# Two more places for expert weights and a 128-row product of the keys' low part, in a two-block transformer kernel

## The chip, the cores and the metric

One Trainium2 chip, one of its cores. The metric is the device time of one execution of the whole program, in microseconds (us); the median of three runs is given for the kernel before. TensorE is called PE below, its weight load PEld, VectorE DVE, ScalarE ACT, GpSimd POOL, and the queue of SyncE, which issues nearly all transfers, SP.

## The reference

256 tokens of width 1024 go through two different transformer blocks, all in float32. What matters here, cut to its core:

```python
# first block: mixer (8 heads + convolution), memory attention, then 32 experts
x = x + parallel_mixer(...); x = x + memory_cross_attention(...)
x = x + hierarchical_moe(h, ...)      # group by softmax, top 2 of its 8 experts
#   every expert: (silu(t @ wg) * (t @ wu)) @ wd, wg and wu 1024x512, wd 512x1024
x = rmsnorm(x, final_g)
# second block: HGRN2 mixer and sparse attention (16 heads of 64, 4 of keys), then
merged = sigmoid(ga) * (y_a @ w_branch_a) + sigmoid(gb) * (y_b @ w_branch_b)
h = h + rms_norm(merged @ w_out, ...)          # then a feed-forward layer and a gated input
# its selected and its window branch, at this length:
s = einsum('bgrqd,bgkd->bgrqk', q_rot, k)      # causal, softmax, times v
```

## The kernel before

The order of the work on each engine is set when the program is built, by a scheduler that gives each tile its place in SBUF and adds the waits; every engine, SP among them, then runs its own list in order. Each part of the first block and of the second is a product of 256 tokens with a weight matrix that arrives in pieces of 1 MB.

**Dense products** (`dense_nat`, `dense_T`). A piece of weights goes to a place of the pool `ring` (4 places), and `wsplit` (L184, L185) turns it into a high part `wh` (ACT, a cast to fp32r) and a low part `wl` (DVE, the rest) in the pool `hl` (3 places of each). The tokens are split the same way (`xTh`, `xTl`). A product is then three fp32r products, high by high, high by low and low by high, all through the helper at L195.

**The experts** (`moe_plan`, `mload`, `moe`). The experts' weights (192 pieces of 1 MB, in groups of four experts: 8 gate, 8 up and 8 down pieces) are used as they come, with no split. `moe_plan` lists the pieces in the order of use, and one row of `final_g` stands in the last group. `mload` puts piece number i into slot i modulo the number of slots. The slots are opened one after another as the first block ends and its tiles go: `NRB` places when the mixer's early tiles are gone, the 4 of `ring`, then `NR2`, `NRC`, `NRE` places, the 3 of `hl` (each holds a piece as two halves, named `wh` and `wl` here too, 512 KB each), and last `NRD`. With 8, 4, 2, 2, 2, 3 and 1 there are 22. The first 22 pieces are therefore loaded while the first block still computes, and each later one when the piece that holds its slot has been used. A product of four experts runs as four column strips (`bg`), and `gather` (`sp`) collects the tokens of the next four. Once, before the second group's loads go on, all engines pass a branch on the number of overflowing tokens (`nov`, L1059 to L1077); the branch holds the only transfers that GpSimd issues at addresses known at run time, and it isn't entered here.

**The second attention** (`att`, within `nsa`). For each of the 16 heads and each half of the queries (`hf`), one PSUM tile `tr` takes the scores of both branches, with 128 keys per branch for the first half and 256 for the second (so 256 and 512 columns). A key tile holds the head's 64 dimensions twice, on partitions 0 to 63 and 64 to 127; `kh` is the high part and `kl` the low part, each copied to the other half by L1503 and L1504. A query tile `qr` holds the high part of the query on one half of the partitions and its low part on the other. Three products go to `tr`:

```python
rr = slice(64 * j, 64 * j + 64)
self.mm(sc, q, kh[g // 2][:, g % 2, :, :kb], True, False)            # 128 rows: (qh + ql) . kh
self.mm(sc, q[rr], kl[g // 2][rr, g % 2, :, :kb], False, False)      # 64 rows: qh . kl
self.mm(sc[:, :, kb - 128:], self.idr, self.cnr[...], False, True)   # causal mask
```

`exps` then takes the maximum (DVE, `anm`) and the exponential (ACT, `P`), `turn` transposes `P` on PE (`hp`, L1547), and `values` multiplies by the values (`po`). The scores of head h, the transposes of head h-1 and the values of head h-2 are written together, and the scheduler sets dense products of the gates and branches between them.

Of the kernel before, what the change touches and what calls it, by code (L numbers as in the profile page):

```python
# [26 lines left out]
WARM = (5, 6, 0, 4, 8, (0, 2, 2, 2), 2, 4)  # L27
PIECES = ((0, 512), (512, 512)), ((0, 512), (512, 256), (768, 256))
ENG = ("VA", "PP", "VA", "VA")
NRB, NR2, NRC, NRE, NRD = 8, 2, 2, 2, 1  # L30
NS4, NPM, NPT, NPA, NHP = 16, 3, 2, 1, 2
ATT = 1300
NHV = 2
# [104 lines left out]
class B:  # L138
# [1212 lines left out]
    def nsa(self, uT, W, s4, b2):  # L1351
        tc, nc, A = self.tc, self.nc, self.A
# [95 lines left out]
        for hf in range(2):  # L1448
            sc = self.pat.tile([128, 16, 15], F32, name="po")
# [32 lines left out]
        kh, kl = ([s4(n, [128, 2, 2, S], F32R) for _ in range(2)] for n in ("kh", "kl"))  # L1482
        vv = []
        for br in range(2):
# [9 lines left out]
            for g2 in range(2):  # L1494
# [3 lines left out]
                for j in range(2):  # L1498
                    r, q = slice(64 * j, 64 * j + 64), slice(64 - 64 * j, 128 - 64 * j)
# [10 lines left out]
        for c, ps in turned(qn):  # L1510
            for j in range(2):
                r, q = slice(64 * j, 64 * j + 64), slice(64 - 64 * j, 128 - 64 * j)
# [4 lines left out]
        def att(ap, pax):  # L1517

            acc, Ps, PTs = {}, {}, {}

            def scores(h):
                g, j = h // 4, h % 2
                if not j:
                    acc[h // 2] = (self.pat.tile([128, 2, 2, 2, 64], F32, name="po"),
                                   self.sm.tile([128, 2, 2, 2], F32, name="asm", bufs=3))
                sm = acc[h // 2][1]
                nm = self.sm.tile([128, 2, 2], F32, name="anm", bufs=2)
                P = Ps[h] = ap.tile([128, 2, 384], F32, name="P", bufs=2)  # L1530
                rr = slice(64 * j, 64 * j + 64)
                for hf, kb, c0 in ((0, 128, 0), (1, 256, 128)):
                    sc = self.ptr.tile([128, 2, kb], F32, name="tr")
                    q = qr[g][:, h % 4, hf * 128:(hf + 1) * 128]
                    self.mm(sc, q, kh[g // 2][:, g % 2, :, :kb], True, False)
                    self.mm(sc, q[rr], kl[g // 2][rr, g % 2, :, :kb], False, False)
                    self.mm(sc[:, :, kb - 128:], self.idr,
                            self.cnr[:, None, :].to_broadcast([128, 2, 128]), False, True)
                    self.exps(sc, P[:, :, c0:c0 + kb], kb, nm[:, hf, :], sm[:, hf, :, j])

            def turn(h):
                P = Ps.pop(h)
                PT = PTs[h] = ap.tile([128, 2, 384], F32, name="PT", bufs=2)
                for br in range(2):
                    pt = pax.tile([128, 384], F32, name="hp")
                    for b in range(3):
                        nc.tensor.transpose(pt[:, b * 128:(b + 1) * 128], P[:, br, b * 128:(b + 1) * 128], idn)  # L1547
                    (V.tensor_copy if br else nc.scalar.copy)(PT[:, br, :], pt)

            def values(h):  # L1550
                g, j = h // 4, h % 2
                po, sm = acc[h // 2]
                PT = PTs.pop(h)
                for br in range(2):
                    v = lambda m: vv[br][:, m, g * 64:(g + 1) * 64]
                    self.mm(po[:, 0, br, j, :], PT[:, br, 0:128], v(0), True, True)
                    self.mm(po[:, 1, br, j, :], PT[:, br, 128:256], v(0), True, False)
                    self.mm(po[:, 1, br, j, :], PT[:, br, 256:384], v(1), False, True)
                if not j:
                    return  # L1560
                rc = self.sm.tile([128, 2, 2, 2], F32, name="arc", bufs=2)
                V.reciprocal(rc, sm)
                V.tensor_tensor(rc, rc, gn[:, :, 1:3, h - 1:h + 1], op=OP.mult)
                tt = self.sm.tile([128, 2, 2, 128], F32, name="att", bufs=2)
                V.tensor_tensor(tt.rearrange("p a b (j d) -> p (a b j) d", j=2), po.rearrange("p a b j d -> p (a b j) d"),
                                rc.rearrange("p a b j -> p (a b j)")[:, :, None].to_broadcast([128, 8, 64]), op=OP.mult)
                for hf in range(2):
                    y = yb[hf][:, (h - 1) * 64:(h + 1) * 64]
                    for br in range(2):
                        V.tensor_tensor(y, y, tt[:, hf, br], op=OP.add)  # L1570

            for h in range(18):
                if h < 16:
                    scores(h)
                if 0 < h <= 16:
                    turn(h - 1)
                if h > 1:
                    values(h - 2)
# [131 lines left out]
```

## Time and profile before

| what | value |
|---|---|
| time, median of 3 runs | 1335.99 us (1333.78 to 1336.66) |
| the profiled execution's own time | 1335.2 us |
| its span | 1333.4 us |
| PE busy | 1222.0 us (92%) |
| DVE, ACT busy | 609.2 us (46%), 482.4 us (36%) |
| data moved | 332.38 MB, 249 GB/s over the span |
| experts' stage | about 280 to 714 us |
| second attention | about 953 to 1058 us |

The span is that of the profiled execution, from its first to its last instruction; its own time lies 1.8 us above it. PE's busy time is partly modelled, so it is read together with the chain of waits, which says what each stretch of the end time hung on.

### The profile page before, as it was taken

The page shows a single profiled execution, that of the slowest core. Times are in us where ns is not written, and L with a number is a line of the kernel's source. Part 1 is how long each engine was busy: PE and PEld are TensorE (multiplying, and loading weights), DVE is VectorE, ACT ScalarE, POOL GpSimd, SP SyncE. Part 2 cuts the span into 40 slices and gives each one's busy share as a digit, 9 for nine tenths or more (in the row PEclk, how much of TensorE's full clock was granted, in tenths as well). Part 3 has the DMA queues.
Part 4 walks back from the last instruction along what each step waited for, and adds up shares of the span by engine and source line. Part 5 has one row for each costly group of instructions (what it writes and reads, how often), then busy time and mean ns, then how long its engine had stood idle before and what let it go on. Part 6 is the DMA issues. An engine that isn't in the chain of part 4 may idle for free.

```text
span 1333.4 us, 17835 instructions
## 1 busy us (share of the span) xinstructions
PE 1222.0 (92%) x7122; PEld 882.0 (66%) x7122; DVE 609.2 (46%) x1031; ACT 482.4 (36%) x916; POOL 130.0 (10%) x171
## 2 busy tenths in 40 slices
PE   8889999989978788796968999999999999999997
PEld 7779888844432323141414998888777878989886
DVE  5897655510100000010004677767656667564665
ACT  5676644300000000000004542345655446454553
POOL 3877000000000000000000000015000000000000
PEclk8999999989999898998989999999999999999999
DMA  8333595769999999999998444633521336555551
GB/s 282 127 127 127 199 379 196 299 249 417 421 417 420 419 417 420 417 420 418 417 407 309 159 158 127 204 129 105 179 95 64 105 132 213 184 196 178 202 190 48
DMA packets 106744, 332.38 MB, mean 249 GB/s; under 512 B 6368, under 2 KB 20512, under 8 KB 86176
## 3 DMA queue, kind: packets, MB, share of 16 engines
q1 hardware_dynamic: 106096, 329.87, 65.7%
q10 hardware_dynamic: 560, 1.31, 0.4%
q8 instruction: 58, 0.95, 0.3%
q14 instruction: 30, 0.25, 0.1%
HBM read 330.11 MB, written 1.05 MB: 248 GB/s over the span
## 4 chain that ended last, share of the span: by engine, by line
PE 48%; DMA 28%; ACT 1%; DVE 1%; issue 0%; DVEq 0%; POOLq 0%; SPq 0%; ACTq 0%
PE mm L195 29%; DMA w<-w_up_in 8%; DMA w<-w_down_in 8%; DMA w<-w_gate_in 7%; PE z L195 7%; PE bg L195 3%; DMA wh<-w_up_in 3%; PE po L195 2%; PE hp L195 2%; PE tr L195 2%; DMA wh<-w_gate_in 1%; PE sp L195 1%; PE hp L1547 1%; DMA w<-w_in_in 0%; ACT wh L184 0%
## 5 line engine op out<-in xcount | busy, mean ns | idle before, releaser
L185 DVE TENSOR_TENSOR wl<-w,wh 128x1024 fp32r<-128x1024 f32 (+2 forms) x228 | 278.9, 1238 | 158.6 <-ACT wh L184 157.4
L184 ACT CAST wh<-w 128x1024 fp32r<-128x1024 f32 (+2 forms) x228 | 235.6, 1044 | 201.7 <-PE mm L195 154.0
L195 PE MATMUL bg<-w,xs 128*32 128x512 f32 x888 | 172.9, 668 | 60.7 <-DMA w<-w_up_in 36.4
L195 PE MATMUL mm<-xTh,wl 128*128 128x256 f32 x688 | 195.6, 289 | 11.1 <-DVE wl L185 11.1
L195 PE MATMUL mm<-xTh,wh 128*128 128x256 f32 x688 | 190.2, 289 | 5.3 <-ACT wh L184 2.8
L195 PE MATMUL mm<-xTl,wh 128*128 128x256 f32 x688 | 193.3, 287 | 0.2 <-DVE xTl L253 0.2
L195 PE MATMUL mm<-wl,xTh 128*128 128x512 f32 (+1 forms) x440 | 173.1, 396 | 0.3 <-DVE wl L185 0.3
L195 PE MATMUL mm<-wh,xTh 128*128 128x512 f32 (+1 forms) x440 | 168.4, 401 | 4.3 <-ACT wh L184 1.3
L195 PE MATMUL mm<-wh,xTl 128*128 128x512 f32 (+1 forms) x440 | 170.3, 394 | 0.0
L195 PEld LDWEIGHTS bg<-w,xs 128*32 128x32 f32 x888 | 38.2, 119 | 179.5 <-issue 77.9
L195 PEld LDWEIGHTS mm<-xTh,wl 128*128 128x128 f32 x688 | 132.5, 193 | 14.1 <-DVE wl L185 13.5
L195 PEld LDWEIGHTS mm<-xTh,wh 128*128 128x128 f32 x688 | 129.6, 193 | 7.9 <-ACT wh L184 3.3
L195 PEld LDWEIGHTS mm<-xTl,wh 128*128 128x128 f32 x688 | 131.8, 193 | 0.8 <-DVE xTl L253 0.4
L988 DVE SCALAR_TENSOR_TENSOR sg<-bg,rsl,sg 128x512 f32<-128x512 f32 x8 | 6.0, 751 | 254.9 <-PE bg L195 254.9
L195 PEld LDWEIGHTS mm<-wh,xTh 128*128 128x128 f32 x440 | 82.4, 189 | 21.9 <-ACT wh L184 1.8
L195 PEld LDWEIGHTS mm<-wl,xTh 128*128 128x128 f32 x440 | 83.1, 189 | 18.0 <-DVE wl L185 1.9
L195 PEld LDWEIGHTS mm<-wh,xTl 128*128 128x128 f32 x440 | 83.0, 189 | 17.8 <-issue 0.7
L195 PE MATMUL bg<-w,ht 128*32 128x512 f32 x456 | 80.0, 598 | 3.5 <-DMA w<-w_down_in 2.8
L195 PEld LDWEIGHTS sp<-oh,X 128*128 128x128 f32 x256 | 61.5, 328 | 12.7 <-issue 10.9
L195 PE MATMUL sp<-oh,X 128*128 128x128 f32 x256 | 65.0, 403 | 0.0
L463 POOL TENSOR_TENSOR zc<-zc,zt 128x256 f32<-128x256 f32 x60 | 63.1, 1052 | 17.3 <-ACT zt L460 12.6
L996 ACT COPY ht<-sp 128x512 f32<-128x512 f32 x8 | 4.7, 586 | 139.8 <-PE sp L994 139.8
(414 smaller groups left out, 1538.2 us busy)
## 6 DMA issues: line engine op xcount, KB each, us to landing
w<-w_down_in SPq DMA_DIRECT2D x73, 1024.0 KB, 16.2
w<-w_up_in SPq DMA_DIRECT2D x68, 1024.0 KB, 15.0
w<-w_gate_in SPq DMA_DIRECT2D x59, 1024.0 KB, 19.9
w<-w_in_in SPq DMA_DIRECT2D x41, 1024.0 KB, 5.3
w<-w_mkv_in SPq DMA_DIRECT2D x8, 1024.0 KB, 5.0
w<-w_out_in SPq DMA_DIRECT2D x8, 1024.0 KB, 5.1
wh<-w_up_in SPq DMA_DIRECT2D x12, 512.0 KB, 17.5
wl<-w_up_in SPq DMA_DIRECT2D x12, 512.0 KB, 13.9
```

The lines of the kernel that those rows point to most:

```text
L184: self.nc.scalar.copy(hv, raw[:, j:j + g, :])
L185: self.nc.vector.tensor_tensor(lv, raw[:, j:j + g, :], hv.bitcast(F32), op=OP.subtract)
L195: return self.nc.tensor.matmul(out, lhsT, rhs, start=start, stop=stop, skip_group_check=True)
L463: nc.gpsimd.tensor_tensor(zi, zi, t, op=OP.add)
L988: V.scalar_tensor_tensor(sg, ps, rsl[q], sg, op0=OP.mult, op1=OP.mult)
L996: nc.scalar.copy(ht, tp)
L1547: nc.tensor.transpose(pt[:, b * 128:(b + 1) * 128], P[:, br, b * 128:(b + 1) * 128], idn)
```

## The change

Two edits. `NRB` goes from 8 to 9 and `NRD` from 1 to 2, so there are 24 slots in place of 22, which is just the number of pieces of four experts; the room comes from a smaller scratch for dynamic transfers. And the score product with the keys' low part takes all 128 rows, which adds the product of the query's low part with the key's low part to the scores.

```diff
-NRB, NR2, NRC, NRE, NRD = 8, 2, 2, 2, 1
+NRB, NR2, NRC, NRE, NRD = 9, 2, 2, 2, 2
...
-                rr = slice(64 * j, 64 * j + 64)
...
-                    self.mm(sc, q[rr], kl[g // 2][rr, g % 2, :, :kb], False, False)
+                    self.mm(sc, q, kl[g // 2][:, g % 2, :, :kb], False, False)
...
-    nc = bacc.Bacc("TRN2", target_bir_lowering=False, num_devices=1)
+    nc = bacc.Bacc("TRN2", target_bir_lowering=False, num_devices=1, dynamic_dma_scratch_size=1024)
```

Lists of DVE and ACT are the same in both kernels; PE's list differs only within the experts' stage, where the down products meet other tiles first. In the second attention no instruction moves on any engine. SP's list of transfers is shown at three places. The first is where the last pieces of the first group are loaded and the first slots are used again, just ahead of the branch (L1059). Before, with two down pieces that wait for PE to give slots back:

```order
L868 DMA wl<-w_down_in 128x1024 [waits DMAHW0_49,PE_49]
L868 DMA w<-w_down_in 128x2048 [waits DMAHW1_49,PE_49]
L868 DMA wh<-w_down_in 128x1024 [waits DMAHW2_49]
L868 DMA w<-w_down_in 128x2048 [waits DMAHW3_49,PE_49]
L868 DMA w<-w_down_in 128x2048 [waits DMAHW4_49,PE_49]
L868 DMA w<-w_gate_in 128x2048 [waits DMAHW5_49,PE_49]
L868 DMA w<-w_gate_in 128x2048 [waits DMAHW6_49,PE_49]
L1059 TENSOR_LOAD nov [waits DVE_49]
```

Now the same place reads:

```order
L868 DMA wl<-w_down_in 128x1024 [waits DMAHW1_49,PE_49]
L868 DMA w<-w_down_in 128x2048 [waits DMAHW2_49,PE_49]
L868 DMA w<-w_down_in 128x2048 [waits DMAHW3_49]
L868 DMA wh<-w_down_in 128x1024 [waits DMAHW4_49]
L868 DMA w<-w_gate_in 128x2048 [waits DMAHW5_49,PE_49]
L868 DMA w<-w_gate_in 128x2048 [waits DMAHW6_49,PE_49]
L868 DMA w<-w_gate_in 128x2048 [waits DMAHW7_49,PE_49]
L868 DMA w<-w_gate_in 128x2048 [waits DMAHW0_49,PE_49]
L1059 TENSOR_LOAD nov [waits DVE_49]
```

All down pieces of the first group now stand ahead of the first reused slot, and the four loads ahead of the branch are the next group's gate pieces. The second place is SP's list where the memory attention's output weights (`w_mo`) are loaded, in the first block. Before:

```order
L868 DMA w<-w_gate_in 128x2048 [waits DMAHW3_49]
L868 DMA w<-w_gate_in 128x2048
L868 DMA w<-w_gate_in 128x2048 [waits DMAHW5_49,PE_49]
L167 DMA w<-w_mo_in 128x4x512 [waits DMAHW6_49,PE_49]
L167 DMA w<-w_mo_in 128x4x512 [waits DMAHW7_49,PE_49]
```

And now, with the ninth early place filled first:

```order
L868 DMA w<-w_gate_in 128x2048 [waits DMAHW3_49]
L868 DMA w<-w_gate_in 128x2048 [waits Pool_49]
L868 DMA w<-w_gate_in 128x2048 [waits DMAHW5_49,PE_49]
L868 DMA w<-w_up_in 128x2048 [waits DMAHW6_49]
L167 DMA w<-w_mo_in 128x4x512 [waits DMAHW7_49,PE_49]
L167 DMA w<-w_mo_in 128x4x512 [waits DMAHW0_49]
```

One more piece of the experts stands ahead of `w_mo`. The third place is SP's list at the end of the experts' stage, with the last down pieces and the first weights of the second block (`w_in`). Before:

```order
L868 DMA w<-w_down_in 128x4x512 [waits DMAHW2_49,PE_49]
L167 DMA w<-w_in_in 128x4x512 [waits DMAHW3_49,PE_49]
L167 DMA w<-w_in_in 128x4x512 [waits DMAHW4_49,PE_49]
L167 DMA w<-w_in_in 128x4x512 [waits DMAHW5_49,PE_49]
L1374 DMA w_5335<-cmp_wk_2_in 128x2x64 [waits DMAHW2_49,DMAHW1_49,DMAHW6_49,DMAHW0_49,PE_49]
L1374 DMA w_5335<-cmp_wv_2_in 128x2x64 [waits DMAHW7_49]
L167 DMA w<-w_in_in 128x4x512 [waits DVE_49]
```

And now:

```order
L868 DMA w<-w_down_in 128x4x512 [waits DMAHW2_49,PE_49]
L167 DMA w<-w_in_in 128x4x512 [waits DMAHW3_49,PE_49]
L167 DMA w<-w_in_in 128x4x512 [waits DMAHW4_49,PE_49]
L167 DMA w<-w_in_in 128x4x512 [waits DMAHW5_49,PE_49]
L167 DMA w<-w_in_in 128x4x512 [waits DMAHW6_49,PE_49]
L1374 DMA w_5335<-cmp_wk_2_in 128x2x64 [waits DMAHW1_49,DMAHW7_49,DMAHW0_49,PE_49]
L1374 DMA w_5335<-cmp_wv_2_in 128x2x64
```

The fourth `w_in` piece no longer waits for DVE, since with 24 slots the row of `final_g` and the last down pieces no longer end up in `ring`; the last pieces that `ring` holds are up pieces.

## Rows read from the trace of the kernel before

**Rows 1.** Busy time by stretch: engines' us (instructions), granted PE clock, DMA share, GB/s.

```profile
203.00:230.00 27.00, 26.95 (x168) 24.51 (x167) 15.42 (x25) 10.99 (x23) 0.00 (x0) 1.00 0.41 144
262.00:278.00 16.00, 16.00 (x96) 11.77 (x98) 5.59 (x30) 1.80 (x4) 0.00 (x0) 1.00 0.13 52
...
300.00:690.00 390.00, 324.03 (x1665) 122.56 (x1669) 23.93 (x46) 15.03 (x27) 0.00 (x0) 0.95 1.01 418
```

**Rows 2.** SP's transfers in order of time: start, us, engine, line, tile.

```profile
188.04 1.27 SPq L167 DMA_DIRECT2D w<-w_mo_in  x2
...
255.94 0.44 SPq L868 DMA_DIRECT2D wh<-w_down_in  x1
278.45 0.80 SPq L868 DMA_DIRECT2D w<-w_down_in  x2
...
700.14 9.48 SPq L167 DMA_DIRECT2D w<-w_in_in  x3
```

**Rows 3.** SP's own waits, 250 to 280 us, then 300 to 730 us: total, times, longest.

```profile
SPq L868 <- PE bg L195: 22.1, 1, 22.1
...
SPq L868 <- PE bg L195: 9.5, 19, 2.2
```

**Rows 4.** Transfers by tile: count, KB each, median us to landing.

```profile
w<-w_down_in SPq DMA_DIRECT2D x73, 1024.0 KB, 16.2
```

**Rows 5.** The chain that ended last, at the end of the experts' stage: start, us.

```profile
697.66 15.42 DMA w<-w_down_in
```

**Rows 6.** ACT in order of time: the first casts of `w_mo` and of `w_in`.

```profile
220.94 2.00 ACT L184 CAST wh<-w 128x1024 fp32r<-128x1024 f32 x2
...
716.02 1.99 ACT L184 CAST wh<-w 128x1024 fp32r<-128x1024 f32 x2 [1.18 <-DMA w<-w_in_in]
```

**Rows 7.** Busy time in the second attention, columns as in Rows 1.

```profile
953.50:1058.50 105.00, 105.00 (x576) 82.79 (x575) 59.48 (x121) 57.64 (x170) 0.00 (x0) 1.00 0.27 91
```

**Rows 8.** The chain that ended last, 950 to 1070 us: shares by line, and one piece.

```profile
by line: PE mm L195 48.6%; PE tr L195 23.3%; PE po L195 16.7%; PE hp L1547 8.8%; PE mm L298 1.5%; PE tr L298 1.3%
...
955.30 4.64 PE mm L195 x20
```

**Rows 9.** PE in order of time, one head's scores: start, us, out<-moving,stationary.

```profile
953.42 0.28 PE L195 MATMUL tr<-kh,qr 128*128 128x256 f32 x1
953.63 0.38 PE L195 MATMUL tr<-kl,qr 64*128 64x256 f32 x1
953.94 0.38 PE L195 MATMUL tr<-cnr,idr 128*128 128x256 f32 x1
954.16 0.40 PE L195 MATMUL tr<-kh,qr 128*128 128x512 f32 x1
954.49 0.49 PE L195 MATMUL tr<-kl,qr 64*128 64x512 f32 x1
954.91 0.39 PE L195 MATMUL tr<-cnr,idr 128*128 128x256 f32 x1
955.13 0.40 PE L195 MATMUL mm<-wl,xTh 128*128 128x512 f32 x1
```

**Rows 10.** PE's weight loads, the first ones of the same head.

```profile
953.63 0.18 PEld L195 LDWEIGHTS tr<-kl,qr 64*128 64x128 f32 x1 [0.25 <-issue]
953.94 0.19 PEld L195 LDWEIGHTS tr<-cnr,idr 128*128 128x128 f32 x1
```

**Rows 11.** A dense product of 128 rows and 256 columns: PE, then its loads.

```profile
744.62 0.29 PE L195 MATMUL mm<-xTh,wh 128*128 128x256 f32 x1
744.74 0.28 PE L195 MATMUL mm<-xTh,wl 128*128 128x256 f32 x1
...
744.62 0.19 PEld L195 LDWEIGHTS mm<-xTh,wl 128*128 128x128 f32 x1
```

**Rows 12.** ACT's last step of one head's `P`, and PE's transposes of it.

```profile
1028.99 0.20 ACT L324 ACTIVATION_READ_ACCUMULATOR P<-tr,anm 128x1 f32 x1
...
1033.15 0.38 PE L1547 MATMUL hp<-cs,P 128*128 128x128 f32 x2
```

## Prediction

> **What bounds the kernel now.** I read busy time by stretch first. From 300 to 690 us the transfers run at a DMA share of 1.01 and 418 GB/s while PE is busy 324 of 390 us [rows 1], so the experts' stage is limited by the bytes still to be loaded when it starts. SP's own waits say the same: in 300 to 730 us it waited for PE to give a slot back 9.5 us in all, 19 times, and the rate did not suffer [rows 3]. The chain of waits ends that stage on a down piece, issued at 697.66 and landed at 713.1 us [rows 5]; the second block follows from there. Just ahead of the stage there is a hole: SP issues the last half piece at 255.94, then waits 22.1 us until PE has used the first slots, and issues again at 278.45 [rows 2, 3]. From 262 to 278 us only 52 GB/s flow [rows 1]. Transfers that had a place to go to could run there.
>
> [...]
>
> **Two more places: a lead of 2 MB.** A piece is 1024 KB, 1.0486 MB [rows 4]; at 418 GB/s it takes 2.51 us. Before, the two last down pieces of the first group go out at 278.45, behind the hole [rows 2]. With 24 slots they need no slot back. The load into the second late place follows that into the first, near 256 us. The ninth early piece goes out ahead of `w_mo`, near 188 us; the queue has room to catch up between 203 and 230 us, where it moves 144 GB/s [rows 1]. Both pieces need 5.0 us, and the hole is 16 us. From 278.45 on there are then two pieces fewer to load: 2 x 2.51 = **5.0 us**. I take all of it. Bounds: 0 if neither lands ahead of 278 us, 5.2 us at the hundredth that the rate could differ plus the issue time.
>
> What else moves costs nothing, under cover that I can name. `w_mo` comes one piece later, 2.5 us: issued at 188.04, cast at 220.94 [rows 2, 6], over 20 us of cover by the queries' product and the memory attention; uncovered it would be 2.5 us. SP issues the same number of transfers. Its wait for PE at 278.45 stays, since PE's first use of slots is no earlier, and the branch behind it passes when it did; PE, ACT and DVE wait there as before. In the steady part a load waits for the piece 24 back rather than 22 back, a weaker condition. The `hl` places now always hold down pieces, as two halves each, still 24 pieces in all. At the end the fourth `w_in` piece goes out with the first three, which before left from 700.14 on [rows 2], ahead of the last landing; the first cast follows the landing of `w_in` at 716.02 [rows 6], 2.9 us behind the last down piece, and I expect the same distance. The smaller scratch serves the branch that is not entered; entered, it would cost what no row here shows.
>
> **The low-part product on 128 rows.** One head's scores [rows 9], start to start: `kh` 0.21, `kl` 0.31, mask 0.22 for the first half, then 0.33, 0.42, 0.22: 1.71 us. Beside that, dense products of 128 rows: 0.12 us for 256 columns [rows 11], and 4.64 us for 20, 0.23 each, for 512 [rows 8]. The difference sits at the change between 128 and 64 rows: the load of `kl`'s stationary tile starts only at 953.63, together with its own product and behind 0.25 us of idle, and the mask's at 953.94 likewise [rows 10], while in the dense product the load for the product at 744.74 starts at 744.62, under the one before it [rows 11]. With all three on 128 rows I expect the dense spacing: 3 x 0.12 + 2 x 0.23 + 0.12 = 0.94 us a head.
>
> All 16 heads: 23.3% of 120 us is 28.0 us [rows 8], 1.75 a head, against 16 x 0.94 = 15.0, so 13.0 us. From that I take off 0.5 us for tiles that follow a float32 product and have a few hundredths that have nothing to do with rows, and 0.5 us for waits that PE may meet when it gets ahead: **12.0 us**. The added low-by-low product rides on rows that the array has anyway; `kh` next to it shows that 128 rows cost no more per column. Who is late next? The steps of a head have slack: ACT ends a head's `P` at 1029.2, PE transposes it at 1033.15 [rows 12], 4 us against 0.8 us that a head gets shorter. DVE would be busy 59.5 of 93 us, 64%. Bounds: 0 below if DVE and ACT give it all back, 13.5 above.
>
> [...]
>
> **Sum.** 5.0 + 12.0 = 17.0 us off the profiled execution: span 1333.4 to 1316.4, its own time 1335.2 to 1318.2. The median of the runs, 1335.99, lies 0.8 us above that execution, so I predict **1319 us**. Later work only shifts: from the attention to the end the chain was PE with no fixed dates in it.
>
> **Rivals.**
> - *Given back in the attention.* PE gets ahead and meets casts of weights or softmax steps of ACT and DVE, which are in order and about 60% busy [rows 7]. For it: a cast can stand behind an exponential. Against: PE waited for nobody in 105 us and the slack above. At half lost: 5 + 6 = 11 us, 1325 us.
> - *Loads stay exposed.* A load could need the running product's end even with 128 rows throughout. The mask's spacing of 0.22 us against 0.12 us [rows 9, 11] puts an exposed load at 0.10 to 0.11. Then a head takes 3 x 0.22 + 2 x 0.33 + 0.22 = 1.54 us and the edit saves 16 x (1.75 - 1.54) = 3.4 us; in all 8.4 us, 1327.6 us. Against it: a load that starts under the product before it [rows 11]. [...]
> - *No lead.* The two pieces only push others, or the last landing waits on something else, and the stage ends when it did: 12 us saved, 1324 us. For it: PE is busy 83% of that stretch and could be late once. Against: 9.5 us of waits in 390 us.
> - *No change.* Neither the rows nor the lead matter: 1336 us. Against: rows 10 for the one, the hole for the other.
> - *Slower.* With 24 slots a slot always meets the same role, and each group's down pieces wait for the down product of the group before, the last thing that PE does with it. If PE came to it too late, the queue would run dry once a group; seven times 3 us costs 21 us, more than both gains, and the time is 1340 us. Some 16.2 / 2.51 = 6.5 pieces are on the way at a time [rows 4], so it decides once PE lags 24 - 6.5 = 17.5 pieces, 44 us, behind the landings. Against: with 22 slots the same count gives 39 us, and SP hardly waits for PE [rows 3].
>
> **Chances and range.** Forecast, 1316 to 1322: 0.60. Given back in part: 0.17. No lead: 0.07. Loads exposed: 0.05. No change: 0.03. Slower: 0.05. Still faster than forecast, below 1316: 0.03. Two parts in a thousand, 2.7 us, is about what a measurement here tells from no change. Faster: 0.60 + 0.17 + 0.07 + 0.05 + 0.03 = 0.92; same 0.03; slower 0.05. The range 1316 to 1326 holds the forecast, the missing lead and three quarters of the partial loss: 0.80. Its lower end is both upper bounds, 5.2 + 13.5, with a run's scatter of a us or so.
>
> **What would show it.** Right: the first group's last two down pieces issued before 260 us, not at 278; the last down piece landing near 708 us; `tr` products 0.12 and 0.23 us apart with loads that start ahead of them; the attention's 105 us near 93 with PE still busy throughout. Wrong: a rate under 415 GB/s between 300 and 690 us or a new wait of SP for PE; score products still over 0.2 us apart for 256 columns; PE waiting for `wl`, `wh` or `P` between 948 and 1045 us.

## The result and the profile after

The changed kernel took 1319.01 us (median of 4 runs, 1318.37 to 1321.18), the kernel before 1336.22 us in the same comparison (4 runs). The ratio is 0.9878, with a 95% interval of 0.9861 to 0.9895: 14 to 19 us faster. The profiled execution's span went from 1333.4 to 1317.3 us. The forecast was 1319 us.

First the busy time by stretch of the changed kernel, in the columns of [rows 1]; the last row is the second attention and answers to [rows 7].

```profile
203.00:230.00 27.00, 26.95 (x170) 24.65 (x169) 15.12 (x23) 11.46 (x23) 0.00 (x0) 1.00 0.50 184
262.00:278.00 16.00, 16.00 (x98) 12.47 (x96) 7.05 (x47) 1.80 (x4) 0.00 (x0) 1.00 0.36 150
300.00:690.00 390.00, 317.58 (x1685) 123.68 (x1686) 24.39 (x46) 15.35 (x28) 0.00 (x0) 0.93 1.01 418
...
948.50:1041.00 92.50, 92.50 (x576) 81.23 (x575) 58.76 (x116) 56.13 (x167) 0.00 (x0) 1.00 0.32 103
```

The hole ahead of the experts' stage now carries 150 GB/s where it carried 52, and the stage runs at the same 418 GB/s. The attention takes 92.5 us with PE busy throughout, as it was over 105.0 us. So both gains are where the prediction's steps put them. SP's transfers in order of time (start, us, line, tile, count) show the first of them:

```profile
188.86 0.94 SPq L167 DMA_DIRECT2D w<-w_mo_in  x2
...
257.17 0.87 SPq L868 DMA_DIRECT2D w<-w_down_in  x2
258.10 0.42 SPq L868 DMA_DIRECT2D wh<-w_down_in  x1
280.13 5.88 SPq L868 DMA_DIRECT2D w<-w_gate_in  x7
...
696.54 12.36 SPq L167 DMA_DIRECT2D w<-w_in_in  x4
```

All down pieces of the first group are issued by 258.10, and what stands behind the wait for PE are gate pieces of the next group, where [rows 2] had two down pieces. SP's own waits for the experts' products, 250 to 285 us and then 300 to 730 us (total, times, longest):

```profile
SPq L868 <- PE bg L195: 23.1, 3, 21.6
...
SPq L868 <- PE bg L195: 9.3, 18, 3.6
```

The wait ahead of the stage stayed, as [rows 3] had it, and in the stage SP waits for PE no more than before in all, though its longest wait is 3.6 us in place of 2.2. The chain that ended last still leaves the stage on a down piece:

```profile
693.93 15.80 DMA w<-w_down_in
```

It lands at 709.73 us, 3.4 us earlier than in [rows 5]; the forecast was 708. The reason is the start: the first reused slot is issued at 280.13, 1.7 us later than in [rows 2]. From there to the last landing it is 429.6 us, against 434.6 before (278.45 to 713.08): the stage is the forecast 5.0 us shorter, and it began late. Why is told in the last section. The first cast of `w_in` follows 2.8 us behind the landing:

```profile
712.56 1.99 ACT L184 CAST wh<-w 128x1024 fp32r<-128x1024 f32 x2 [1.07 <-DMA w<-w_in_in]
```

In the attention, PE in order of time, one head's scores, the same place as [rows 9]:

```profile
949.80 0.28 PE L195 MATMUL tr<-kh,qr 128*128 128x256 f32 x1
949.91 0.28 PE L195 MATMUL tr<-kl,qr 128*128 128x256 f32 x1
950.03 0.28 PE L195 MATMUL tr<-cnr,idr 128*128 128x256 f32 x1
950.16 0.39 PE L195 MATMUL tr<-kh,qr 128*128 128x512 f32 x1
950.39 0.39 PE L195 MATMUL tr<-kl,qr 128*128 128x512 f32 x1
950.62 0.28 PE L195 MATMUL tr<-cnr,idr 128*128 128x256 f32 x1
950.74 0.40 PE L195 MATMUL mm<-wl,xTh 128*128 128x512 f32 x1
```

From 949.80 to 950.74 the six products take 0.94 us, where they took 1.71. The weight loads of the same products stand one product ahead, and none has the idle time that the first of [rows 10] had:

```profile
949.80 0.19 PEld L195 LDWEIGHTS tr<-kl,qr 128*128 128x128 f32 x1
949.92 0.19 PEld L195 LDWEIGHTS tr<-cnr,idr 128*128 128x128 f32 x1
```

The load for `kl` starts at 949.80, with `kh`'s product and 0.11 us ahead of its own. The chain's shares from 930 to 1070 us, by line:

```profile
by line: PE mm L195 63.4%; PE po L195 14.3%; PE tr L195 11.1%; PE hp L1546 7.5%; PE tr L298 1.9%; PE mm L298 1.3%; PE tr L1427 0.6%
```

The score tiles hold 11.1% of 140 us, 15.5 us, against 28.0 before.

### The profile page after: what moved, and what is told of

It is laid out like the page before. It is cut to its first block, busy times and chain, and to the rows that moved or that the text cites. A ratio compares the mean times of both kernels' runs of the same rounds, so it can differ in the third digit from the quotient of the medians.

```text
span 1317.3 us, 17827 instructions
## 1 busy us (share of the span) xinstructions
PE 1199.9 (91%) x7122; PEld 881.4 (67%) x7122; DVE 609.2 (46%) x1031; ACT 482.1 (37%) x916; POOL 130.1 (10%) x171
## 4 chain that ended last, share of the span: by engine, by line
PE 49%; DMA 27%; ACT 1%; DVE 1%; issue 0%; SPq 0%; DVEq 0%; POOLq 0%; ACTq 0%
PE mm L195 29%; DMA w<-w_up_in 10%; DMA w<-w_gate_in 9%; PE z L195 7%; DMA w<-w_down_in 4%; PE bg L195 3%; PE po L195 2%; PE hp L195 2%; DMA wl<-w_down_in 2%; PE sp L195 2%; DMA wh<-w_down_in 1%; PE tr L195 1%; PE hp L1546 1%; DMA w<-w_in_in 0%; ACT wh L184 0%
## 5 line engine op out<-in xcount | busy, mean ns | idle before, releaser
L195 PE MATMUL bg<-w,xs 128*32 128x512 f32 x1024 | 177.0, 702 | 71.1 <-DMA w<-w_up_in 50.9
L195 PE MATMUL bg<-w,ht 128*32 128x512 f32 x320 | 69.3, 597 | 2.5 <-DMA w<-w_down_in 1.8
L463 POOL TENSOR_TENSOR zc<-zc,zt 128x256 f32<-128x256 f32 x60 | 63.1, 1053 | 17.2 <-ACT zt L460 12.4
## 6 DMA issues: line engine op xcount, KB each, us to landing
wh<-w_down_in SPq DMA_DIRECT2D x24, 512.0 KB, 16.1
```

Source lines behind the costliest of these rows:

```text
L195: return self.nc.tensor.matmul(out, lhsT, rhs, start=start, stop=stop, skip_group_check=True)
L463: nc.gpsimd.tensor_tensor(zi, zi, t, op=OP.add)
```

## The experiments

Times below are medians, each beside runs of the kernel before on the same chip. Single runs of one kernel differ by up to 7 us on one chip, and medians of one kernel by up to 2, so the sizes are read from three marks of each profile: SP's issue into the first reused slot, PE's first score product of the second attention, and PE's first transpose of the gate `sga` behind it (L298). All columns are in us.

| kernel | first reused slot | first score | first `sga` | slot to score | score to `sga` |
|---|---|---|---|---|---|
| before | 278.45 | 953.42 | 1080.43 | 674.97 | 127.01 |
| rows alone | 278.22 | 953.13 | 1067.75 | 674.91 | 114.62 |
| places alone | 279.34 | 948.45 | 1075.46 | 669.11 | 127.01 |
| early place alone | 277.37 | 950.49 | 1077.50 | 673.12 | 127.01 |
| all on 64 rows | 278.53 | 953.34 | 1078.49 | 674.81 | 125.15 |
| after | 280.13 | 949.80 | 1064.41 | 669.67 | 114.61 |
| after, again | 278.87 | 949.08 | 1063.68 | 670.21 | 114.60 |
| after, timed again | 276.98 | 946.86 | 1061.46 | 669.88 | 114.60 |
| after, gap filled | 278.41 | 946.80 | 1061.42 | 668.39 | 114.62 |
| after, gap filled, timed again | 278.20 | 947.17 | 1061.79 | 668.97 | 114.62 |
| after without the low part | 277.40 | 946.53 | 1056.15 | 669.13 | 109.62 |

**The rows alone.**

```diff
-                    self.mm(sc, q[rr], kl[g // 2][rr, g % 2, :, :kb], False, False)
+                    self.mm(sc, q, kl[g // 2][:, g % 2, :, :kb], False, False)
```

> The kernel before with the low-part product on 128 rows and nothing else; every engine's list is that of before, row for row. Theory (the cost sits at the change between 128 and 64 rows): the attention takes 92.5 us in place of 105.0 as in the profile after, so 12.4 us off the median, about 1323.8 us. Rival 1 (the two edits help each other, and part of the attention's gain came from the places): under 10 us off, over 1326 us. Rival 2 (part of the places' gain is eaten by something that the rows bring): over 14 us off, under 1322 us.

Measured: 1324.91 us against 1336.44, ratio 0.9919 (0.9900 to 0.9937), 8.4 to 13.4 us off. By the marks, score to `sga` is 12.4 us shorter and slot to score the same to 0.1 us. The attention in this run, columns as above:

```profile
953.00:1045.50 92.50, 92.50 (x576) 81.23 (x575) 58.83 (x119) 57.05 (x170) 0.00 (x0) 1.00 0.32 103
```

It is the 92.5 us of the changed kernel, to the hundredth. The interval holds the theory's 12.4; it doesn't exclude rival 1's bound by itself, the marks do.

**The places alone.**

```diff
-NRB, NR2, NRC, NRE, NRD = 8, 2, 2, 2, 1
+NRB, NR2, NRC, NRE, NRD = 9, 2, 2, 2, 2
...
+    nc = bacc.Bacc("TRN2", target_bir_lowering=False, num_devices=1, dynamic_dma_scratch_size=1024)
```

> The kernel before with the two more places and the smaller scratch, the low-part product on 64 rows as before; every engine's list is that of after but for that product. Theory: 5.0 us off the experts' stage from its first reused slot to its last landing (434.6 us before, 429.6 after), and the 1.7 us by which the stage began late in the profile after belong to that execution: first reused slot near 278.5 us, median 5 us below before, about 1331.2 us. Rival 1 (the extra piece ahead of the stage costs those 1.7 us every time): first reused slot near 280.1 us, 3.3 us below before, about 1332.9 us. Rival 2 (the places give nothing by themselves): within 1 us of before.

Measured: 1331.76 us, ratio 0.9958 (0.9943 to 0.9973), 3.6 to 7.6 us off. Slot to score is 5.9 us shorter, the attention unchanged. The stretches 262 to 278 and 948.5 to 1053.5 us:

```profile
262.00:278.00 16.00, 16.00 (x94) 11.96 (x91) 6.32 (x38) 1.80 (x4) 0.00 (x0) 1.00 0.31 130
...
948.50:1053.50 105.00, 105.00 (x576) 82.78 (x575) 59.47 (x121) 57.66 (x170) 0.00 (x0) 1.00 0.27 91
```

So the two edits add up: by the ratios 10.8 and 5.6 us, 16.4 together, against 16.3 for both at once (0.0122 of 1336), each with 2 us or more to either side. The marks say it more sharply: each edit shortens its own column and leaves the other's within 0.1 us. But the stage began late here too, at 279.34, which spoke for rival 1 until the changed kernel was run again (below).

**The early place alone (23 slots).**

```diff
-NRB, NR2, NRC, NRE, NRD = 8, 2, 2, 2, 1
+NRB, NR2, NRC, NRE, NRD = 9, 2, 2, 2, 1
...
+    nc = bacc.Bacc("TRN2", target_bir_lowering=False, num_devices=1, dynamic_dma_scratch_size=1024)
```

> As the run with the places alone, but with the ninth early place only (23 slots). Theory (each MB loaded ahead is worth its 2.51 us at the stage's rate of 418 GB/s): half the gain, 2.5 us below before, about 1333.7 us, stage 432.1 us from first reused slot to last landing. Rival (what counts is that 24 slots are the pieces of just four experts): with 23 nothing is gained, 1336.2 us, or all 5 come with one place, 1331.2 us.

Measured: 1334.60 us, ratio 0.9988 (0.9979 to 0.9998), 0.3 to 2.8 us off; slot to score 1.85 us shorter. One place gives something, and not the whole: both forms of the rival fall, and the theory's 2.5 us comes out 0.65 us short. The end of the stage shows why. First the issue of the last down piece, its time to landing (the last figure of the second row), and the granted clock from 700 to 705 us; then PE's rows (start, us, out<-in; the idle time ahead and its releaser in brackets):

```profile
694.13 2.03 SPq L868 DMA_DIRECT2D w<-w_down_in  x1
w<-w_down_in SPq DMA_DIRECT2D x1, 1024.0 KB, 15.4
...
700.00:705.00 5.00, 4.26 (x8) 1.17 (x4) 0.69 (x1) 1.27 (x3) 0.00 (x0) 0.50 1.05 390
```

```profile
698.74 1.86 PE L195 MATMUL bg<-w,ht 128*32 128x512 f32 x8 [2.97 <-DMA w<-w_down_in]
701.33 3.78 PE L195 MATMUL mm<-od,pt 128*128 128x512 f32 x4 [0.74 <-ACT od L1019]
705.04 2.22 PE L195 MATMUL bg<-w,ht 128*32 128x512 f32 x16
...
710.31 1.06 PE L195 MATMUL bg<-w,ht 128*32 128x512 f32 x8
```

The last down piece landed at 709.5 us, 432.2 us behind the first reused slot, as the theory had it (432.1). But behind 705.04 PE waits for no transfer any more, and it begins its product with that piece only at 710.31, 0.8 us behind the landing; in the kernel before it began 0.04 us behind it. So here the stage ends on PE, not on a landing, and that is where the missing 0.65 us went. From 700 to 705 us PE's granted clock was 0.50, after a wait of 2.97 us, and the four products took 3.78 us. In the changed kernel's first profile, with a granted clock of 1.00 from 700 to 705 us, the same four took 1.98 us:

```profile
700.73 1.98 PE L195 MATMUL mm<-od,pt 128*128 128x512 f32 x4 [0.74 <-ACT od L1019]
```

The 1.8 us between them are more than the 0.8 us by which PE was late; that the clock made it late is read from these rows, no run changed the clock here. The changed kernel's second profile shows the same: 3.68 us for the four, the last product 0.9 us behind its landing, and the longest slot to score of the five with 24 slots and the gap unfilled, 670.21. To the last landing the stage goes from 434.7 us (the mean of three profiles with 22 slots) over 432.2 with 23 to 429.5 with 24 (the mean of those five): 2.5 and 2.7 us a place. That leaves nothing for the smaller scratch, which was not run alone.

**All three products on 64 rows.**

```diff
-                    self.mm(sc, q, kh[g // 2][:, g % 2, :, :kb], True, False)
+                    self.mm(sc, q[rr], kh[g // 2][rr, g % 2, :, :kb], True, False)
...
-                    self.mm(sc[:, :, kb - 128:], self.idr,
-                            self.cnr[:, None, :].to_broadcast([128, 2, 128]), False, True)
+                    self.mm(sc[:, :, kb - 128:], self.idr[rr],
+                            self.cnr[rr, None, :].to_broadcast([64, 2, 128]), False, True)
```

> The kernel before with all three score products on 64 rows: the product with the high part leaves out the query's low part, and the mask product leaves out half of the mask's rows. Every engine's list is that of before, row for row, so PE goes from 128 to 64 rows and back 31 times in place of 32, with 96 products on 64 rows in place of 32. Theory (a change of rows costs about 0.40 us there and back, 64 rows as such cost nothing): 0.4 to 1 us below before, about 1335.5 us. Rival (each 64-row product costs about 0.2 us in its own load, wherever it stands, two of them a group more): 32 x 0.4 = 12.8 us above before, about 1349 us.

Measured: 1334.64 us, ratio 0.9986 (0.9976 to 0.9997), 0.4 to 3.2 us off; score to `sga` 1.86 us shorter. The rival, which forecast 12.8 us more, falls. PE, and then two of its weight loads, at the place of [rows 9]:

```profile
953.01 0.40 PE L195 MATMUL mm<-wh,xTh 128*128 128x512 f32 x1
953.34 0.38 PE L195 MATMUL tr<-kh,qr 64*128 64x256 f32 x1
953.56 0.28 PE L195 MATMUL tr<-kl,qr 64*128 64x256 f32 x1
953.68 0.28 PE L195 MATMUL tr<-cnr,idr 64*128 64x256 f32 x1
953.80 0.39 PE L195 MATMUL tr<-kh,qr 64*128 64x512 f32 x1
954.03 0.39 PE L195 MATMUL tr<-kl,qr 64*128 64x512 f32 x1
954.26 0.28 PE L195 MATMUL tr<-cnr,idr 64*128 64x256 f32 x1
954.47 0.50 PE L195 MATMUL mm<-wl,xTh 128*128 128x512 f32 x1
```

```profile
953.34 0.18 PEld L195 LDWEIGHTS tr<-kh,qr 64*128 64x128 f32 x1 [0.37 <-issue]
953.45 0.19 PEld L195 LDWEIGHTS tr<-kl,qr 64*128 64x128 f32 x1
```

Between 64-row products the spacing is the dense one, 0.12 us for 256 columns and 0.23 for 512, and the load of `kl` starts 0.11 us ahead of its product. Time is lost only on the way in (the first load starts behind 0.37 us without one, and two spacings of 0.33 and 0.22 us stand where 0.23 and 0.12 would) and on the way out (0.21 where 0.12 would). It is the change of the row count that costs, not the 64 rows. The 1.86 us are more than the 0.4 to 1 us expected, because a way there and back came out a little cheaper here behind a float32 product, such as a transpose of `P`: from that transpose to the dense product behind the scores (first half of the second head) it is 0.89 us before, 0.83 here and 0.50 in the changed kernel. What PE does between the two row counts isn't shown. The rows show that the first load behind the step from 128 to 64 rows starts only with its own product (both at 953.34), and so does the first behind the step back (954.46, its product at 954.47); the size, there and back, is 0.39 us for the kernel before (below).

**The changed kernel again.** No edit.

> The changed kernel once more, for its clock near 232 us. In six executions looked at, PE has the same two gaps there, 1.12 and 0.50 us, while it waits for the memory attention's softmax on DVE; the granted clock then fell to 0.50 for about 3 us in the two kernels with both new places and in none of the four others. Theory (the fall is a matter of the execution, not of the places): it may stay at 1.00 here, and the experts' first reused slot then comes near 278.5 to 279.2 us. Rival (the places bring the fall): 0.50 again near 234 us, first reused slot near 279.3 to 280.1 us. One execution can only speak for the theory by staying at 1.00; a fall would leave the two about as they are.

Measured: 1318.22 us in this one execution. Granted clock from 232 to 236 us (the third figure from the end), first in the changed kernel's first profile, then in this one:

```profile
232.00:234.00 2.00, 1.18 (x5) 0.87 (x6) 1.57 (x6) 1.70 (x5) 0.00 (x0) 0.86 1.02 416
234.00:236.00 2.00, 2.00 (x8) 1.73 (x7) 2.00 (x3) 0.00 (x0) 0.00 (x0) 0.50 1.00 418
```

```profile
232.00:234.00 2.00, 1.36 (x9) 1.05 (x10) 1.57 (x6) 1.52 (x4) 0.00 (x0) 1.00 1.05 426
234.00:236.00 2.00, 1.74 (x8) 1.13 (x8) 1.98 (x3) 0.00 (x0) 0.00 (x0) 1.00 1.03 430
```

The same kernel, the same two gaps ahead of it (1.12 and 0.50 us), and the clock stayed at 1.00; the first reused slot came at 278.87. The rival, that the places bring the fall, is out in the form "every time"; that they make it more likely is not.

**The gap filled.**

```diff
                         V.reciprocal(mr[:, hf, h2:h2 + 2], ms[:, hf, h2:h2 + 2])
+                        if h2:
+                            self.busy(ms[:, hf, h2:h2 + 2], self.cs[:, :256], (4, 2)[hf])
```

> The changed kernel with six products added that nothing reads (the sums of the memory attention's softmax, two columns, against 256 columns), which PE gets right at the gap near 231 us; they use the time in which it waits for DVE. At 0.27 us each, the spacing of the products with 256 columns at L729, they fill 1.6 us. Theory (the fall of the clock follows the gap): granted clock 1.00 from 228 to 240 us, first reused slot near 279 us, up to 1.1 us off the median, which is less than it can show. Rival (the fall has another cause, or the added products delay the transposes behind them): 0.50 again, or the stage starts later than 280.1 us.

Measured: 1316.69 us, ratio 0.9854 (0.9836 to 0.9872), clock 1.00 from 228 to 238 us, first reused slot 278.41. The added products stretch over 2.75 us in the trace, more than the 1.6 us expected. The time lay 2.3 us below the changed kernel's first median, from other rounds, so both were timed again on one chip:

> The changed kernel once more, timed beside the run below on the same chip. Both theories: about 17 us below before, 1318 to 1320 us; its clock near 232 us may stay at 1.00 or fall, since it stayed at 1.00 in one execution and fell in another.

> The changed kernel with the six products that fill the gap near 231 us, as before, now timed beside the changed kernel itself. Theory (the fill is worth more than the fall that it prevents, since the stage began at 278.41 us and ended 3 us sooner in the one profile): 2 us or more below the changed kernel in the same rounds. Rival (those 3 us are mostly that one execution's own clock elsewhere): within 1 us of the changed kernel.

Measured: 1317.22 us for the changed kernel (ratio 0.9870, 0.9851 to 0.9888) and 1317.30 us with the gap filled (0.9869, 0.9852 to 0.9885), against 1335.49. The first lies a little under the 1318 to 1320 us expected of it. There is no difference between the two: the rival held, and the fill is worth nothing that these runs can show. In both profiles the clock stayed at 1.00 there, so they don't test whether the fill prevents the fall either.

**Without the low part.**

```diff
-                    self.mm(sc, q, kl[g // 2][:, g % 2, :, :kb], False, False)
```

> The changed kernel without the product of the keys' low part: the scores of the second attention leave it out. Two products a head fewer, 0.12 and 0.23 us apart on 128 rows; the scheduler then sets some dense products of that stretch in another order. Theory (PE alone sets the pace in the attention, and there is slack left on DVE and ACT): 16 x 0.35 = 5.6 us off, attention near 87 us, median about 1313.5 us. Rival 1 (at 92.5 us the softmax steps were about to be late): PE waits in this stretch, under 3 us off, over 1316 us. Rival 2 (the low product on 128 rows still costs more than its columns): over 8 us off, under 1311 us.

Measured: 1312.39 us, ratio 0.9820 (0.9803 to 0.9836), 7.7 us below the changed kernel's first ratio and 6.7 below its second. Between the two profiles an earlier first slot makes 2.7 us and slot to score 0.5 us, which the edit doesn't touch; score to `sga` gives 5.0 us of the expected 5.6. PE's waits from 930 to 1060 us and the stretch up to 1034 us show where the rest went:

```profile
PE hp L1545 <- ACT P L324: 0.4, 1, 0.4
```

```profile
946.50:1034.00 87.50, 87.33 (x545) 76.54 (x543) 60.09 (x118) 56.46 (x165) 0.00 (x0) 1.00 0.36 118
```

For the first time in these runs PE waits for `P` in the attention, once, for 0.4 us. In the changed kernel it waits for nobody there. So the slack of ACT and DVE sufficed for the change, and a further 5.0 us meet a first, short wait. Both rivals fall, rival 1 with 0.4 us of waits and rival 2 with the 5.0 us. Whether still more would be lost was not tried, and the dense products stand in another order here.

## Why the prediction was right, step by step

**The lead, 5.0 us.** Right in size and mechanism. From first reused slot to last landing the stage is 5.0 us shorter in the first pair of profiles, and 5.2 by the means above (434.7 and 429.5). From first reused slot to first score, five profiles with 24 slots and the gap unfilled take 669.6 us on average, three with 22 slots 674.9, so 5.3 us; with the two filled ones it is 5.6. What the step didn't see is that a stage's own start moves by up to 3 us between executions (276.98 to 280.13), so the landing was forecast at 708 and came at 709.73 in the one profile shown. "No lead" falls with the run of the places alone, "slower" with SP's 9.3 us of waits for PE in the stage.

**What else moves, nothing.** Right as far as the rows go: `w_mo` was issued at 188.86 in place of 188.04, no new wait of PE for its casts shows between 185 and 262 us, the rate stayed at 418 GB/s, and the distance to the first cast behind the stage is 2.8 us in place of 2.9.

**The rows, 12.0 us.** 12.4 in every pair of profiles. PE was busy throughout the stretch before (105.0 us) and after (92.5 us), so what it saved was time of the kernel. The spacing is the forecast one, 0.94 us a head. The first half us taken off, for tiles behind a float32 product, was right (the score tiles hold 15.5 us, where 16 x 0.94 is 15.0); the second, for waits that PE might meet, wasn't needed: it met none, so "given back" falls. Spread over 32 changes of rows, 12.4 us is 0.39 us for each way there and back.

"Loads stay exposed" would have left 3.4 us of this edit. The loads of the 128-row score products start one product ahead of their own, behind rows of the same kind (949.80 for the product at 949.91, as 744.62 for 744.74 in [rows 11]), and the run of the rows alone gave 12.4.

**The sum.** 17.0 us forecast; the marks give 5.3 + 12.4 = 17.7, the first profile 16.1 (span, with its late start), the medians 17.2 and, in the second timing, 18.3. That the first median met the forecast to a hundredth of a us is luck: the terms came out 0.7 us larger, and the kernel's own scatter is larger still.

## What to carry to other kernels

The score products, which switched between 128 and 64 rows, paid for the switch here (0.33 to 0.39 us for each way there and back), not for the rows (0.12 us for 256 columns on either): where a trace shows the same, put products of one kind side by side, or spend the unused half of the rows on a harmless extra term. In this stage, which ran at 418 GB/s from 300 to 690 us, room for one more piece was worth 2.5 to 2.7 us, about that piece's 2.51 us at the stage's rate; there was a hole of 16 us ahead of the stage in which it could land, and with 23 slots, where the stage ended on PE and not on a landing, the gain from slot to score came out 0.65 us short. When two edits sit in different stages, marks at the stages' borders tell their sizes apart, here to a few hundredths of a us in the attention and to about 1 us in the stage of the transfers, where the intervals of the medians leave 4 to 5 us open.

## What the runs showed that was not expected

The granted clock falls behind the same gap in one execution and not in another. The two gaps near 231 us (1.12 and 0.50 to 0.51 us in all nine profiles in which they were not filled) were followed by about 3 us at a granted clock of about 0.50 in two of them, the changed kernel's first (0.73, 0.50, 0.50 and 0.56 in the four us from 233 to 237) and the places alone (0.80, then three times 0.50, from 232 to 236), and by 1.00 throughout in seven. Both are among the five with 24 slots; two in five against none in four is too few to tell whether that matters. PE's rows in the changed kernel's first profile show the price:

```profile
233.41 1.53 PE L656 MATMUL tr<-cs,P 128*128 128x128 f32 x6 [0.50 <-DVE P L647]
234.59 1.20 PE L195 MATMUL mm<-wh,xTh 128*128 128x512 f32 x2
...
238.50 3.61 PE L195 MATMUL po<-PT,mV 128*128 128x256 f32 x16
```

and, in the same kernel's second profile:

```profile
233.23 0.88 PE L656 MATMUL tr<-cs,P 128*128 128x128 f32 x6 [0.50 <-DVE P L647]
233.86 0.72 PE L195 MATMUL mm<-wh,xTh 128*128 128x512 f32 x2
...
237.26 3.61 PE L195 MATMUL po<-PT,mV 128*128 128x256 f32 x16
```

From the start of the six transposes to that of the two products behind them it is 1.18 us against 0.63, and to the products with the values (`po`) 5.09 against 4.03. So the fall costs 1.1 us. The first profile's stage began 1.7 us later than before: 1.1 us of it are this, and by 0.6 us PE was late already at the gap (its first transposes there start at 232.32, before at 231.72). Where those 0.6 us come from is open; in the nine profiles the same transposes start between 230.24 and 232.32. A second such place is a gap of 2.04 us in the second block (near 1105 us in the changed kernel): the 25 us around it had a granted clock of 0.93 in the four profiles of one chip (rows alone, places alone, early place, all on 64 rows) and 1.00 in the seven others, and from the first `sga` to the end of the span those four take 254.5 us, the seven 252.8 to 253.0. So 1.5 us of the rows-alone profile, whose span fell by 11.2 us in place of 12.7, went there. Whether the chip, its state or the moment decides was not settled.
